# Where the row statistics stand, and how many operand tiles there are: six tiles more, a quarter of the DMA scratch

## The chip, the cores and the metric

The kernel runs on one core of a Trainium2 chip. The metric is device time in microseconds (us) for one execution, from a run of the whole program; 1877.57 us is the median of three runs of the kernel before (1875.49 to 1882.97). On the core, TensorE (PE) multiplies matrices, VectorE (DVE) and ScalarE (ACT) do the elementwise work, GpSimd (POOL) and SyncE (SP) mostly issue DMAs.

## The reference

Five layers in a row on 512 rows of width 1024, all in float32: a SwiGLU feed-forward (ffn1), a mixer of two attentions, a second feed-forward (ffn2), an mLSTM and an RG-LRU, then a last norm. Every layer begins with the same RMS norm and a product with its first weights:

```python
def rms_norm(x, g):
    xf = x.astype(jnp.float32)
    y = xf * lax.rsqrt(jnp.mean(xf * xf, axis=-1, keepdims=True) + EPS)
    return (y * g.astype(jnp.float32)).astype(x.dtype)

def swiglu(x, w_gate, w_up, w_down):
    return (jax.nn.silu(x @ w_gate) * (x @ w_up)) @ w_down

# first block
h = h + 0.5 * swiglu(rms_norm(h, ffn1_norm), ...)
u = rms_norm(h, mix_norm); z = u @ w_in            # two attentions, two gated branches
h = h + merged @ w_out
h = h + 0.5 * swiglu(rms_norm(h, ffn2_norm), ...)
x = rms_norm(h, final_norm)
# second block
x = x + mlstm_mixer(rmsnorm(x, ln_g[0]), ...)
x = x + rglru_mixer(rmsnorm(x, ln_g[1]), ...)
return rmsnorm(x, final_g)

# in mlstm_mixer, of each of 4 heads:
xc = jax.nn.silu(causal_dwconv(xm, conv_w, conv_b))   # 4 taps along the rows
q, k = xc @ w_q, xc @ w_k
v = xm @ w_v
```

## The kernel before

Activations lie transposed: a tile is 128 features by 512 rows. A float32 product is made of three: both sides are split into a rounded part `hi` and a rest `lo`, and `mm3` issues hi·hi (L113), hi·lo (L114) and lo·hi (L115). A `group` is one weight tile of 128x1024 against eight activation tiles, 24 matmuls of 128x512 into one PSUM tile; `bank` and `cbank` are two pools of four such tiles.

The norm is not applied before the first product. `operand` splits x times the gain, without the row factor; the factor 1/rms of each row, spread over all partitions as the tile `rb`, is multiplied in when a product leaves PSUM (L197, L354, L418, L785, L1027). The way to `rb`: `sumsq` squares on ACT, adds on DVE and sums over partitions in four PE matmuls (L171); `rstd` is one DVE instruction (L178) and one power on POOL (L179); `rows` is four PE transposes (L185) and a DVE copy (L187). `stats` does all of that at once, after the first three or four groups of a layer (the mLSTM, which needs two such sums, has the same steps written out after three).

In the feed-forwards most products are done in 256-wide halves by a scheme with fewer products (`xhalves`, `pair_products`): `xhalves` makes seven operands for each of four steps from `x`, the gain and `rb` (L271 to L285). Their weights are sums of weight tiles; one summand comes by an accumulating DMA that POOL issues (L212, 36 of them), all other loads are issued by SP.

In the mLSTM each head needs the convolved, activated input, tile by tile (`x_conv`): one DVE instruction with the first tap (L989), three more (L992), a tanh on ACT (L795), a DVE multiply (L796), then `split`: a cast on ACT (L122) and a subtraction on DVE (L124). The operand, its cast, its rest and the convolution's own temporaries all come out of one pool, `ap`, of tiles of 128x512 float32 with the name `act`: 2 KB in each partition, 34 of them.

The order on each engine is not written out. The framework orders the instructions by priority (offsets of 75 for weights, 100 for evacuations, 200 for `operand`), by the order of the code and by the pools: an instruction that takes a tile from a full pool waits until the last reader of the oldest tile is done, on whatever engine that is. So a pool's size changes the order on all engines. SBUF is full: the pools and the scratch that the program sets aside for the dynamic DMAs (the software ones, which are POOL's) share it.

Of the kernel before, what the change touches and what calls it, by code (L numbers as in the profile page):

```python
# [42 lines left out]
def kernel(ctx: ExitStack, tc: tile.TileContext, a, out):  # L43
    nc = tc.nc
# [1 line left out]

    cp = ctx.enter_context(tc.tile_pool(name="cp", bufs=1))
    op = ctx.enter_context(tc.tile_pool(name="op", bufs=1))
    ap = ctx.enter_context(tc.tile_pool(name="ap", bufs=34))
    wp = ctx.enter_context(tc.tile_pool(name="wp", bufs=5))  # L50
    sp = ctx.enter_context(tc.tile_pool(name="sp", bufs=32))
    gp = ctx.enter_context(tc.tile_pool(name="gp", bufs=2))
# [7 lines left out]
    def act_tile(dt=F32):  # L60
        return ap.tile([P, T], dt, tag="act", name="act")

    def bank():
        return pp.tile([P, T], F32, tag="bank", name="bank")

    def ctile(dt=F32):
        return xp.tile([P, T], dt, tag="chain", name="chain")

    def cbank():
        return qp.tile([P, T], F32, tag="cbank", name="cbank")  # L70

    def small(n):
        return sp.tile([P, 16], F32, tag="small", name="small")[:, :n]

    def f(t):
        return t.bitcast(F32)
# [3 lines left out]
    def vc(name, i=0, n=None):  # L80
        o, w = VEC[name]
        return vec[:, o + i : o + i + (1 if n is None else n)]
# [10 lines left out]
    def wload(src, cols=WU):  # L93
        with tc.high_priority(offset=BOOST):
            raw = wp.tile([P, WU], F32, tag="raw", name="raw", bufs=4)
            nc.sync.dma_start(raw[:, :cols], src)
            hi = wp.tile([P, WU], F32R, tag="hi", name="hi")
            S.copy(hi[:, :cols], raw[:, :cols])  # L98
            lo = wp.tile([P, WU], F32R, tag="lo", name="lo")
            V.tensor_tensor(lo[:, :cols], raw[:, :cols], f(hi[:, :cols]), op=ALU.subtract)  # L100
        return hi, lo
# [10 lines left out]
    def mm3(ps, st, mv, start, stop):  # L112
        PE.matmul(ps, st[0], mv[0], start=start, stop=False)  # L113
        PE.matmul(ps, st[0], mv[1], start=False, stop=False)  # L114
        PE.matmul(ps, st[1], mv[0], start=False, stop=stop)  # L115

    def cut(pair, sl):
        return pair[0][:, sl], pair[1][:, sl]

    def split(x, mk=act_tile):  # L120
        hi = mk(F32R)
        S.copy(hi, x)  # L122
        lo = mk(F32R)
        V.tensor_tensor(lo, x, f(hi), op=ALU.subtract)  # L124
        return hi, lo

    def rowcol(t):
        return t.rearrange("p (r c) -> p r c", c=64)

    def colrow(t):  # L130
        return t.rearrange("p (c r) -> p r c", r=8)

    def operand(x, gain, perm=False):
        xs = []
        for k in range(KD):
            hi, lo = act_tile(F32R), act_tile(F32R)
            xi, hv, lv = (rowcol(x[k]), colrow(hi), colrow(lo)) if perm else (x[k], hi, lo)
            with tc.high_priority(offset=200):
                S.activation(hv, xi, AF.Copy, scale=gain[:, k : k + 1])
                V.scalar_tensor_tensor(lv, xi, gain[:, k : k + 1], f(hv), op0=ALU.mult, op1=ALU.subtract)  # L140
            xs.append((hi, lo))
        return xs

    def group(w, xs, ps=None, start=True, stop=True, base=0):
        if ps is None:
            ps = bank()
        n = len(xs)
        for k in range(n):
            c = (base + k) * P
            mm3(ps, cut(w, slice(c, c + P)), xs[k], start and k == 0, stop and k == n - 1)  # L150
        return ps

    def sumsq(x, perm=False, gain=None, fuse=False):
        acc = None
        for k in range(KD):
            sq = ctile()
            S.activation(sq, x[k], AF.Square, scale=1.0 if gain is None else gain[:, k : k + 1])
            if k == KD - 1:
                if fuse:
                    break  # L160
                t = ctile() if perm else sq
                v = (colrow(t), rowcol(sq), rowcol(acc)) if perm else (t, sq, acc)
                V.tensor_tensor(*v, op=ALU.add)
                sq = t
            elif k:
                V.tensor_tensor(sq, sq, acc, op=ALU.add)
            acc = sq
        ps = cbank()
        for b in range(4):
            c = slice(b * P, (b + 1) * P)  # L170
            PE.matmul(ps[:, b : b + 1], acc[:, c], ones[:, :1], start=True, stop=not fuse)  # L171
            if fuse:
                PE.matmul(ps[:, b : b + 1], sq[:, c], ones[:, :1], start=False, stop=True)
        return ps[:, :4]

    def rstd(ms):
        rs = small(4)
        V.tensor_scalar(rs, ms, 1.0 / D, EPS, op0=ALU.mult, op1=ALU.add)  # L178
        G.tensor_tensor(rs, rs, mhalf[:, :4], op=ALU.pow)  # L179
        return rs  # L180

    def rows(rs):
        ps = cbank()
        for b in range(4):
            PE.transpose(ps[:, b * P : (b + 1) * P], rs[:, b : b + 1].to_broadcast([P, P]), ident)  # L185
        rb = rp.tile([P, T], F32, tag="rb", name="rb")
        V.tensor_copy(rb, ps)  # L187
        return rb

    def stats(x, perm=False):  # L190
        rs = rstd(sumsq(x, perm))
        return rs, rows(rs)

    def silu2(ps, rb):
        g = act_tile()
# [147 lines left out]
    def ffn(x, gain, gu, dn, pre=None):  # L343
        xs = operand(x, gain)
        pre = pre or [wload(gu[0])]
        pre = [group(pre[n] if n < len(pre) else wload(gu[n]), xs, (bank if n < 2 else cbank)()) for n in range(4)]
        _, rb = stats(x)

        def plain(j):
            pg, pu = pre[2 * j : 2 * j + 2] if j < 2 else [group(wload(gu[2 * j + i]), xs) for i in range(2)]  # L350
            s = silu2(pg, rb)
            u = act_tile()
            with tc.high_priority(offset=EVAC):
                V.tensor_tensor(u, pu, rb, op=ALU.mult)  # L354
            V.tensor_tensor(u, u, s, op=ALU.mult)
            return split(u)

        def down(o, w, base, us):
            ps = group(w, us, base=base)
            with tc.high_priority(offset=EVAC):  # L360
                V.scalar_tensor_tensor(x[o], ps, 0.25, x[o], op0=ALU.mult, op1=ALU.add)

        def down_two(o, k0):
            c = slice(k0 * P, k0 * P + T)
            with tc.high_priority(offset=BOOST):
                raw = raw_load([dn[o][:, c], dn[o + 1][:, c]], None)
                return wsplit(raw)

        b, step = xhalves(x, gain, rb)
        pr = [plain(0), plain(1)]  # L370
        for k in range(4):
            step(k)
        pr += [plain(2), plain(3)]
        def down_job(j):

            if j >= 20:
                return lambda i: None
            o, got, us = 2 * (j % 4), [], old

            def step(i):  # L380
                if i < 0:
                    got.append(down_two(o, 4 * (j // 4 - 1)))
                else:
                    down(o + i, got[0], 4 * i, us)

            return step

        cur = Pair(gu[8], gu[9])
        cur.load()
        cur.first()  # L390
        cur.sums()
        cur.last()
        old, new = pr, []
        for j in range(4, KF):
            nxt = Pair(gu[2 * j + 2], gu[2 * j + 3]) if j + 1 < KF else None
            job = down_job(j)
            job(-1)
            new.append(pair_products(cur, b, nxt, job))
            cur = nxt
            if j % 4 == 3 and j < 19:  # L400
                old, new = new, []
        for o in range(KD):
            dw = wload(dn[o][:, 16 * P :], 6 * P)
            down(o, dw, 0, new)
# [4 lines left out]
    def mixer(x):  # L409
        xs = operand(x, vc("gm", 0, 8), perm=True)  # L410
        win = a["win"]
        pre = [group(wload(win[4 * (n % 2) + n // 2]), xs, (bank if n < 2 else cbank)()) for n in range(4)]
        rs, rb = stats(x, perm=True)
        def q_group(i):
            ps = pre[2 * i] if i < 2 else group(wload(win[i]), xs)
            t = act_tile()
# [292 lines left out]
    def mlstm(x):  # L709
        g0 = small(8)  # L710
        V.tensor_tensor(g0, vc("gf", 0, 8), vc("l0", 0, 8), op=ALU.mult)
        xs = operand(x, g0)
        psf = group(wload(a["mif"]), xs, cbank())
        pre = [group(wload(a["mh"][0][j]), xs) for j in range(2)]
        s1 = sumsq(x)
        s2 = sumsq(x, gain=vc("gf", 0, 8))
        rs1 = rstd(s1)
        ms = small(4)
        V.tensor_tensor(ms, rs1, rs1, op=ALU.mult)
        V.tensor_tensor(ms, ms, s2, op=ALU.mult)  # L720
        rs = rstd(ms)
# [3 lines left out]
        rb = rows(rs)  # L725
# [271 lines left out]

    def rglru(x):
        xs = operand(x, vc("l1", 0, 8))
        pre = [group(wload(a["rxr"][j]), xs, (bank if j < 2 else cbank)()) for j in range(3)]  # L1000
        _, rb = stats(x)
        bah, bxh = small(12), small(12)
        V.tensor_scalar(bah, vc("rba", 0, 12), 0.5, None, op0=ALU.mult)
        V.tensor_scalar(bxh, vc("rbx", 0, 12), 0.5, None, op0=ALU.mult)
# [111 lines left out]
    rs = rstd(ms)  # L1116
# [134 lines left out]
```

## Time and profile before

| what | value |
|---|---|
| median of 3 runs | 1877.57 us (1875.49 to 1882.97) |
| profiled execution | 1878.55 us, of which the span is 1876.8 |
| PE busy | 1816.8 us, 97% of the span |
| DVE, ACT, POOL busy | 69%, 42%, 3% |
| granted PE clock, mean | 0.985 of full speed |
| ffn1, mixer, ffn2, mLSTM, RG-LRU | from about 0, 375, 725, 1087 and 1624 us |

The span is the time from the first to the last instruction of the profiled execution, 1.75 us less than its own time. Times in rows count from the span's start. A matmul's row shows its length in the pipeline; what it costs a full engine is the distance from its start to the next one's.

### The profile page before, as it was taken

To read this page: it belongs to the slowest core of one execution; us is meant where nothing else is said; L and a number is where in the kernel's file an instruction comes from. 1 tells how busy PE (TensorE), PEld (TensorE's weight loads), DVE (VectorE), ACT (ScalarE), POOL (GpSimd) and SP (SyncE) were. 2 spreads that over 40 slices of the span, in tenths; PEclk is the share of its full clock that TensorE was granted. 3 is DMA by queue.
4 is the path that set the end of the run, shared out by engine and by line. 5 is a ranking of instruction groups with operands and counts; after the bars stand their busy time and mean duration, and the time that the engine had idled before them with its cause. 6 is when DMAs were issued, how large, how long until landed. Compare 5 with 4: busy or idle time off the path is not lost.

```text
span 1876.8 us, 24687 instructions
## 1 busy us (share of the span) xinstructions
PE 1816.8 (97%) x9616; PEld 1528.2 (81%) x9616; DVE 1287.1 (69%) x2056; ACT 795.4 (42%) x1190; POOL 64.8 (3%) x89
## 2 busy tenths in 40 slices
PE   7999999999999999999999998799999999999998
PEld 5799999877776688799999886687887888888786
DVE  6987778825555464987777766567466466787785
ACT  4443334523344433444333443334334334447662
POOL 0000000000000000000000000000000000000000
PEclk9999999999999999999999999899999999999999
DMA  7265555423321133265555422122222222222212
GB/s 221 85 174 151 152 152 133 143 85 107 96 79 57 57 101 104 68 171 153 152 152 135 127 92 69 55 80 78 78 91 79 79 93 69 95 94 90 87 60 79
DMA packets 74805, 198.09 MB, mean 106 GB/s; under 512 B 8000, under 2 KB 8128, under 8 KB 74688
## 3 DMA queue, kind: packets, MB, share of 16 engines
q1 hardware_dynamic: 63024, 174.35, 28.4%
q0 software_dynamic: 9792, 18.88, 6.3%
q10 hardware_dynamic: 1872, 3.29, 0.6%
q8 instruction: 75, 1.23, 0.3%
q14 instruction: 42, 0.34, 0.1%
HBM read 193.08 MB, written 2.10 MB: 104 GB/s over the span
## 4 chain that ended last, share of the span: by engine, by line
PE 78%; issue 13%; DVE 6%; ACT 2%; DMA 1%; POOL 1%; SPq 0%; POOLq 0%; ACTq 0%; DVEq 0%
PE bank L113 20%; PE bank L114 20%; PE bank L115 19%; PE cbank L114 4%; PE cbank L113 4%; PE cbank L115 4%; PE cbank L869 1%; PE cbank L636 1%; PE cbank L604 1%; DVE act L992 1%; DMA raw<-in_gu_dram 1%; PE cbank L893 1%; ACT hi L98 1%; DVE act L271 1%; PE cbank L894 1%
## 5 line engine op out<-in xcount | busy, mean ns | idle before, releaser
L113 PE MATMUL bank<-act,hi 128*128 128x512 f32 (+1 forms) x1656 | 625.2, 379 | 32.3 <-ACT act L122 24.8
L114 PE MATMUL bank<-act,hi 128*128 128x512 f32 (+1 forms) x1656 | 623.9, 377 | 1.2 <-DVE act L140 0.7
L115 PE MATMUL bank<-act,lo 128*128 128x512 f32 (+1 forms) x1656 | 620.2, 375 | 1.3 <-DVE lo L100 1.3
L98 ACT CAST hi<-raw 128x1024 fp32r<-128x1024 f32 (+2 forms) x211 | 213.3, 1014 | 427.5 <-PE bank L114 241.3
L113 PEld LDWEIGHTS bank<-act,hi 128*128 128x128 f32 x1656 | 316.1, 191 | 93.4 <-ACT act L122 28.2
L114 PEld LDWEIGHTS bank<-act,hi 128*128 128x128 f32 x1656 | 316.2, 191 | 60.0 <-DVE act L124 4.0
L115 PEld LDWEIGHTS bank<-act,lo 128*128 128x128 f32 x1656 | 316.0, 191 | 57.4 <-issue 1.9
L100 DVE TENSOR_TENSOR lo<-raw,hi 128x1024 fp32r<-128x1024 f32 (+2 forms) x211 | 248.1, 1177 | 152.7 <-ACT hi L98 151.8
L218 ACT CAST hi<-raw 128x1024 fp32r<-128x1024 f32 x140 | 146.4, 1050 | 246.8 <-PE cbank L114 108.7
L220 DVE TENSOR_TENSOR lo<-raw,hi 128x1024 fp32r<-128x1024 f32 x140 | 170.6, 1224 | 78.4 <-ACT hi L218 78.4
L113 PE MATMUL cbank<-chain,hi 128*128 128x256 f32 x432 | 123.3, 286 | 2.5 <-ACT chain L122 2.3
L114 PE MATMUL cbank<-chain,hi 128*128 128x256 f32 x432 | 122.9, 285 | 2.2 <-DVE chain L124 2.2
L115 PE MATMUL cbank<-chain,lo 128*128 128x256 f32 x432 | 122.7, 284 | 0.0
L114 PE MATMUL cbank<-act,hi 128*128 128x256 f32 (+1 forms) x264 | 88.2, 334 | 2.2 <-DVE act L124 2.2
L113 PE MATMUL cbank<-act,hi 128*128 128x256 f32 (+1 forms) x264 | 88.5, 335 | 1.5 <-ACT act L122 1.3
L114 PE MATMUL bank<-lo,act 128*128 128x512 f32 x224 | 88.3, 394 | 0.0
L113 PE MATMUL bank<-hi,act 128*128 128x512 f32 x224 | 88.2, 394 | 0.0
L113 PEld LDWEIGHTS cbank<-chain,hi 128*128 128x128 f32 x432 | 83.5, 193 | 5.2 <-ACT chain L122 3.2
L115 PE MATMUL bank<-hi,act 128*128 128x512 f32 x224 | 87.7, 392 | 0.0
L115 PE MATMUL cbank<-act,lo 128*128 128x256 f32 (+1 forms) x264 | 87.7, 332 | 0.0
L114 PEld LDWEIGHTS cbank<-chain,hi 128*128 128x128 f32 x432 | 83.1, 193 | 4.6 <-DVE chain L124 3.1
L115 PEld LDWEIGHTS cbank<-chain,lo 128*128 128x128 f32 x432 | 83.3, 193 | 0.1
(274 smaller groups left out, 2583.1 us busy)
## 6 DMA issues: line engine op xcount, KB each, us to landing
raw<-in_mh_dram SPq DMA_DIRECT2D x64, 512.0 KB, 3.5
raw<-in_gu_dram SPq DMA_DIRECT2D x52, 512.0 KB, 3.6
raw<-in_gu_dram SPq DMA_DIRECT2D x72, 256.0 KB, 2.9
raw<-in_gu_dram POOLq DMA_DIRECT2D x36, 512.0 KB, 6.1
raw<-in_win_dram SPq DMA_DIRECT2D x34, 512.0 KB, 3.5
raw<-in_dn_dram SPq DMA_DIRECT2D x64, 256.0 KB, 2.9
v<-in_gu_dram SPq DMA_DIRECT2D x36, 256.0 KB, 2.8
raw<-in_mo_dram SPq DMA_DIRECT2D x16, 512.0 KB, 3.5
```

The source lines that it names most:

```text
L98: S.copy(hi[:, :cols], raw[:, :cols])
L100: V.tensor_tensor(lo[:, :cols], raw[:, :cols], f(hi[:, :cols]), op=ALU.subtract)
L113: PE.matmul(ps, st[0], mv[0], start=start, stop=False)
L114: PE.matmul(ps, st[0], mv[1], start=False, stop=False)
L115: PE.matmul(ps, st[1], mv[0], start=False, stop=stop)
L218: S.copy(hi, raw)
L220: V.tensor_tensor(lo, raw, f(hi), op=ALU.subtract)
L271: V.scalar_tensor_tensor(t, x[i], gain[:, i : i + 1], rb, op0=ALU.mult, op1=ALU.mult)
L604: PE.matmul(ps[:, :n], bq[i][ro, nb * P : nb * P + P], bk[0][ro, b0 * P : b1 * P], start=True, stop=True)
L636: PE.matmul(po[64 * g : 64 * g + 64, :], bv[0][:, kb * P + 64 * g : kb * P + 64 * g + 64], ptc, start=kb == b0, stop=kb == b1 - 1)
L869: PE.matmul(ps[:, :n], qk[2 + k][:, s * P : s * P + P], qk[k][:, s * P :], start=k == 0, stop=k == 1)
L893: PE.matmul(ps[:, :256], wh, vl[:, c0 : c0 + 256], start=False, stop=False)
```

## The change

`dynamic_dma_scratch_size=4096` is given where nothing was given before (16384 bytes); the 12 KB of each partition that this leaves make six more `act` tiles, 34 to 40. `stats` goes, and `opening` comes: it issues two groups, then the squares and 1/rms, then the third group, then the transposes and the copy, then the fourth group. ffn, mixer and RG-LRU call it (the last made three groups before, and now four); the mLSTM, whose first group is that of its gates, is written out in the same manner, with both of its sums after one more group and then two more groups.

```diff
-    ap = ctx.enter_context(tc.tile_pool(name="ap", bufs=34))
+    ap = ctx.enter_context(tc.tile_pool(name="ap", bufs=40))
...
-    def stats(x, perm=False):
+    def opening(make, x, perm=False):
+
+        gs = [make(0), make(1)]
         rs = rstd(sumsq(x, perm))
-        return rs, rows(rs)
+        gs.append(make(2))
+        rb = rows(rs)
+        gs.append(make(3))
+        return gs, rs, rb
...
         pre = pre or [wload(gu[0])]
-        pre = [group(pre[n] if n < len(pre) else wload(gu[n]), xs, (bank if n < 2 else cbank)()) for n in range(4)]
-        _, rb = stats(x)
+        ws = pre
+        pre, _, rb = opening(lambda n: group(ws[n] if n < len(ws) else wload(gu[n]), xs, (bank if n < 2 else cbank)()), x)
...
-        pre = [group(wload(win[4 * (n % 2) + n // 2]), xs, (bank if n < 2 else cbank)()) for n in range(4)]
-        rs, rb = stats(x, perm=True)
+        pre, rs, rb = opening(lambda n: group(wload(win[4 * (n % 2) + n // 2]), xs, (bank if n < 2 else cbank)()), x, True)
...
         psf = group(wload(a["mif"]), xs, cbank())
-        pre = [group(wload(a["mh"][0][j]), xs) for j in range(2)]
+        pre = [group(wload(a["mh"][0][0]), xs)]
         s1 = sumsq(x)
         s2 = sumsq(x, gain=vc("gf", 0, 8))
+        pre += [group(wload(a["mh"][0][j]), xs) for j in (1, 2)]
...
-        pre = [group(wload(a["rxr"][j]), xs, (bank if j < 2 else cbank)()) for j in range(3)]
-        _, rb = stats(x)
+        pre, _, rb = opening(lambda j: group(wload(a["rxr"][j]), xs, (bank if j < 2 else cbank)()), x)
...
-    nc = bacc.Bacc("TRN2", target_bir_lowering=False, num_devices=1)
+    nc = bacc.Bacc("TRN2", target_bir_lowering=False, num_devices=1, dynamic_dma_scratch_size=4096)
```

Lines of the kernel after are numbered five higher from L197 on: L989, L992, L796, L212 become L994, L997, L801, L217.

On POOL, at the start of ffn1, the kernel before has two accumulating DMAs ahead of the power of `rstd`:

```order
masks.py:199 AFFINE_SELECT ident<-ident 128x128
L212 DMA raw<-in_gu_dram 128x2x512 x2
L179 TENSOR_TENSOR small<-small,mhalf 128x4
L212 DMA raw<-in_gu_dram 128x2x512 x16
L179 TENSOR_TENSOR small<-small,mhalf 128x4
```

The same place in the kernel after:

```order
masks.py:199 AFFINE_SELECT ident<-ident 128x128
L179 TENSOR_TENSOR small<-small,mhalf 128x4
L217 DMA raw<-in_gu_dram 128x2x512 x18
L179 TENSOR_TENSOR small<-small,mhalf 128x4
L588 MEMSET chain 128x384
```

The power stands ahead of all accumulating DMAs of its layer; the number of these is the same. In ffn2 one of them stays ahead of it where there were two. On PE, L171 stands in ffn1 behind 48 matmuls where there were 96, and L185 behind 72 where there were 104.

On DVE, in the mLSTM's first head, the kernel before has its third and fourth convolution tile (each begins with L989) behind the scaling of the attention's transposed columns (L871):

```order
L871 TENSOR_SCALAR chain<-chain,gT 128x128
L989 TENSOR_SCALAR act<-act,vec 128x512 [waits DVE_49,PE_49]
L992 SCALAR_TENSOR_TENSOR act<-act,vec 128x511 [waits DVE_49]
L992 SCALAR_TENSOR_TENSOR act<-act,vec 128x510 [waits DVE_49]
L992 SCALAR_TENSOR_TENSOR act<-act,vec 128x509 [waits DVE_49]
L796 SCALAR_TENSOR_TENSOR act<-act 128x512 [waits Activation_49]
L124 TENSOR_TENSOR act<-act 128x512 [waits PE_49,Activation_49]
L989 TENSOR_SCALAR act<-act,vec 128x512 [waits DVE_49,PE_49]
```

The same two tiles in the kernel after (they begin with L994):

```order
L124 TENSOR_TENSOR act<-act 128x512 [waits Activation_49]
L994 TENSOR_SCALAR act<-act,vec 128x512
L100 TENSOR_TENSOR lo<-raw,hi 128x1024 [waits DMAHW7_49,Activation_49]
L997 SCALAR_TENSOR_TENSOR act<-act,vec 128x511 [waits DVE_49]
L997 SCALAR_TENSOR_TENSOR act<-act,vec 128x510 [waits DVE_49]
L997 SCALAR_TENSOR_TENSOR act<-act,vec 128x509 [waits DVE_49]
L801 SCALAR_TENSOR_TENSOR act<-act 128x512 [waits Activation_49]
L187 COPY rb<-cbank 128x512 [waits PE_49]
L124 TENSOR_TENSOR act<-act 128x512 [waits Activation_49]
L994 TENSOR_SCALAR act<-act,vec 128x512
```

The first instruction of each tile no longer waits for PE, and both tiles stand ahead of the residual's eight scalings (L772, now L777) or among them. The second tile has moved up too: its L994 and its L997s now stand between the scans of the gates (L756 to L759).

On DVE, in the second head, the last of the four convolution tiles before:

```order
L989 TENSOR_SCALAR act<-act,vec 128x512 [waits PE_49]
L992 SCALAR_TENSOR_TENSOR act<-act,vec 128x511 [waits DVE_49]
L992 SCALAR_TENSOR_TENSOR act<-act,vec 128x510 [waits DVE_49]
L863 COPY chain<-cbank 128x512 [waits PE_49]
L992 SCALAR_TENSOR_TENSOR act<-act,vec 128x509 [waits DVE_49]
L871 TENSOR_SCALAR chain<-chain,gT 128x512 [waits DVE_49]
```

and in the kernel after:

```order
L994 TENSOR_SCALAR act<-act,vec 128x512
L997 SCALAR_TENSOR_TENSOR act<-act,vec 128x511 [waits DVE_49]
L997 SCALAR_TENSOR_TENSOR act<-act,vec 128x510 [waits DVE_49]
L997 SCALAR_TENSOR_TENSOR act<-act,vec 128x509 [waits DVE_49]
L801 SCALAR_TENSOR_TENSOR act<-act 128x512 [waits Activation_49]
L124 TENSOR_TENSOR act<-act 128x512 [waits Activation_49]
L868 COPY chain<-cbank 128x512 [waits PE_49]
```

The wait for PE is gone from its first instruction, and the copy from PSUM (L863, now L868) stands behind the whole tile. The third head has the same difference; the fourth had no such wait before. The number of instructions on PE, DVE, ACT, POOL and SP is the same in both kernels.

## Rows read from the trace of the kernel before

**Rows 1.** The page: the span, and busy time of the engines.

```profile
span 1876.8 us, 24687 instructions
...
PE 1816.8 (97%) x9616; PEld 1528.2 (81%) x9616; DVE 1287.1 (69%) x2056; ACT 795.4 (42%) x1190; POOL 64.8 (3%) x89
```

**Rows 2.** Waits of PE, whole span: total us, times, longest us.

```profile
PE bank L113 <- ACT act L122: 24.8, 6, 6.7
...
PE cbank L185 <- POOL small L179: 5.5, 4, 2.6
...
PE cbank L185 <- DVE small L722: 0.9, 1, 0.9
```

**Rows 3.** Timeline, PE, 1159 to 1196: start, length, instruction [idle before <-releaser].

```profile
1159.93 0.48 PE L113 MATMUL bank<-act,hi 128*128 128x512 f32 x1
...
1162.77 0.60 PE L861 MATMUL cbank<-ident,cT 128*128 128x128 f32 x4
1170.08 2.07 PE L113 MATMUL bank<-act,hi 128*128 128x512 f32 x4 [6.71 <-ACT act L122]
...
1179.82 0.80 PE L113 MATMUL bank<-act,hi 128*128 128x512 f32 x1 [4.87 <-ACT act L122]
...
1189.94 0.80 PE L113 MATMUL bank<-act,hi 128*128 128x512 f32 x1 [4.86 <-ACT act L122]
...
1195.09 0.39 PE L113 MATMUL bank<-hi,act 128*128 128x512 f32 x1
```

**Rows 4.** Timeline, DVE, same stretch.

```profile
1162.94 0.54 DVE L989 TENSOR_SCALAR act<-act,vec 128x512 f32<-128x512 f32 x1
...
1174.77 0.55 DVE L989 TENSOR_SCALAR act<-act,vec 128x512 f32<-128x512 f32 x1 [1.88 <-PE bank L114]
```

**Rows 5.** Stages: us, busy PE, PEld, DVE, ACT, POOL, PEclk, DMA, GB/s.

```profile
60.00:76.00 16.00, 12.01 (x62) 9.85 (x62) 15.56 (x29) 8.37 (x15) 0.66 (x1) 0.79 0.11 34
390.00:400.00 10.00, 8.26 (x36) 6.55 (x35) 4.51 (x7) 1.05 (x1) 1.98 (x1) 0.83 0.28 101
770.00:787.00 17.00, 12.71 (x65) 10.90 (x64) 16.20 (x33) 8.33 (x15) 0.25 (x1) 0.80 0.10 32
1145.00:1163.00 18.00, 17.51 (x89) 14.01 (x90) 9.56 (x14) 6.71 (x9) 0.00 (x0) 1.00 0.23 81
1160.00:1198.00 38.00, 21.56 (x63) 14.89 (x61) 23.50 (x36) 13.01 (x21) 1.26 (x8) 0.73 0.09 28
1302.00:1318.00 16.00, 12.09 (x39) 8.37 (x38) 9.23 (x15) 7.83 (x14) 1.59 (x4) 0.79 0.14 40
```

**Rows 6.** Timeline, PE, second head, 1302 to 1316.

```profile
1308.69 0.80 PE L113 MATMUL bank<-act,hi 128*128 128x512 f32 x1 [3.92 <-ACT act L122]
...
1314.17 0.40 PE L113 MATMUL bank<-hi,act 128*128 128x512 f32 x1
```

**Rows 7.** Timeline, DVE, second head.

```profile
1302.79 0.55 DVE L989 TENSOR_SCALAR act<-act,vec 128x512 f32<-128x512 f32 x1 [3.54 <-PE bank L114]
```

**Rows 8.** Timeline, POOL, ffn1.

```profile
36.78 1.21 POOL L212 DMA_DIRECT2D raw<-in_gu_dram  x1 [7.92 <-DMA raw<-in_gu_dram]
37.54 1.52 POOL L179 TENSOR_TENSOR small<-small,mhalf 128x4 f32<-128x4 f32 x1
```

**Rows 9.** Timeline, PE, ffn1.

```profile
39.12 0.65 PE L185 MATMUL cbank<-ident,small 128*128 128x128 f32 x4 [2.61 <-POOL small L179]
```

**Rows 10.** Timeline, DVE, ffn1.

```profile
39.81 0.69 DVE L187 COPY rb<-cbank 128x512 f32<-128x512 f32 x1 [3.93 <-PE cbank L185]
...
51.72 1.41 DVE L271 SCALAR_TENSOR_TENSOR act<-h,vec,rb 128x512 f32<-128x512 f32 x2
```

**Rows 11.** Instructions of line L212: its DMAs' time to landing.

```profile
DMA to landing us min/median/max: 5.7/6.1/9.2
```

**Rows 12.** Timeline, POOL, ffn1's products.

```profile
120.10 1.20 POOL L212 DMA_DIRECT2D raw<-in_gu_dram  x1 [10.56 <-DVE lo L220]
```

**Rows 13.** Timeline, ACT, same place.

```profile
127.47 1.05 ACT L218 CAST hi<-raw 128x1024 fp32r<-128x1024 f32 x1 [3.03 <-PE bank L114]
```

## The prediction

> **What bounds the kernel now.** I read the page's busy times first. PE is busy for 1816.8 of 1876.8 us [rows 1]; the next engine has 69%. So the chain of work is PE's, and its idle 60 us are what an edit of order can win, with one addition: what PE's clock loses around the idle. Second I read who PE waits for [rows 2]. The reader is to see how few waits there are: six for a cast of an operand tile on ACT (L122) hold 24.8 us, four for the power of the row statistics on POOL 5.5, one more in the mLSTM's opening 0.9. Third, the timeline where the long ones stand: three of 6.71, 4.87 and 4.86 us in the mLSTM's first head, each ahead of one convolution tile's 12 matmuls [rows 3], and one of 3.92 in the second head [rows 6]; the third head repeats it. Last, the table of stages [rows 5]: in the two feed-forward openings (60 to 76 and 770 to 787) DVE is busy for 15.56 of 16 and 16.20 of 17 us while PE stands for 3.99 and 4.29, so there PE waits for the seven operands of each half step, which DVE makes too late.
>
> The clock stands in the same table. [...] In matmuls: twelve at the full clock took from 1159.93 to 1162.77, 0.237 us each [rows 3]; the 36 of the three tiles took 4.87, 5.26 and 5.15 us between the waits (each end is the next start less its wait), 15.28 where 36 x 0.237 make 8.53. So the first head loses 16.44 by waits and 6.75 by the clock, 23.2 us. The second loses 3.92 and (5.48 from 1308.69 to 1314.17, less 12 x 0.237) 2.64, together 6.6 [rows 6], and the third as much.
>
> **The convolution tiles (pool of 40).** Why the casts are late: the tile's first DVE instruction, L989, waits for PE [rows 4, 7]. The tile it writes belongs to PE's last reader of an older one, so a tile's convolution begins when the matmuls of the tile before end, and its chain of about 5 us (1174.77 to 1179.82) stands open to PE. The arithmetic is unchanged; with six more tiles that wait is gone in the new order, and the second to fourth tile move up. What comes late next is DVE's own time. One tile costs it 0.55 + 2.32 + two of 0.69, some 4.2 us. Two tiles move into the stretch before 1163, where DVE is busy for 9.56 of 18 us [rows 5]: 8.4 us of work meet 8.4 us of room, a full fit. The second stands between the gates' scans, so PE's transposes of these are late by up to its four instructions, about 2.8 us; in the order they stand behind some ten more matmuls (2.4 us), so nearly nothing of that shows. The fourth tile shares DVE with the residual; laid one behind the other, its cast ends at about 1168.6 and its rest at 1169.8, and PE, which goes on at 1162.8 with 36 matmuls of 0.237, wants them at about 1168.6 and 1169. I take 22 of the 23.2 us; the bounds are 16.4 (the waits go, the clock doesn't come back) and 23.2. In the second head DVE can begin the last tile where its 3.54 us of idle began, 1299.25 [rows 7]: three L992 after it, tanh, multiply and cast bring the cast to about 1304.1, the rest to 1304.9. PE gets there at 1304.2 (its transposes L861 now stand behind). I take 6.0 of 6.6 us, and the same in the third: 12 us, bounds 7.8 and 13.2.
>
> [...]
>
> **The openings.** The edit removes no instruction; it moves the chain from the squares to `rb` ahead of one or two groups, and draws one RG-LRU group ahead of the evacuations. In ffn1 the chain was held twice: L171 stood behind four whole groups, and the power stood on POOL behind an accumulating DMA that waited for its own load until 36.78 [rows 8]; PE then waited 2.61 us [rows 9]. Now L185 stands 32 matmuls earlier (7.6 us) and the power ahead of the DMAs, so `rb` is done about 10 us sooner than 39.81 [rows 10]. Queued behind the power on POOL is now the layer's first accumulating DMA; the power is done before 30 by this, and the DMA waited for its load anyway. The first half step (L271) began 11.9 us after `rb` [rows 10], behind evacuations, some of which still wait for PE's groups; I let the steps come 8 to 10 us sooner. PE reaches their products 2.6 us sooner, so of the 3.99 us of waits I keep 1.5, and of the clock's part 0.5: the low clock lasted 0.21 x 16 x 2 = 6.7 us, some 5 of them busy, which cost 2.5. Gain: 2.6 + 2.5 + 2.0 = 7.1, of which I take 6.1, because the weights' splits (L220) are pushed behind the steps on a full DVE; bounds 2.6 and 9.1. ffn2: waits of 4.29, and 2.5 for a low clock of the same length (0.20 x 17 x 2 = 6.8); I take 5.3 of 6.8, bounds 2 and 6.8. Mixer: 1.74 us idle (390 to 400 [rows 5]) and half of the 3.4 us at the low clock (0.17 x 10 x 2), 1.7; the sums stand far ahead in the new order: 3.4, bounds 1.7 and 3.4. The four waits for POOL hold 5.5 us [rows 2]; ffn1's 2.61 and the mixer's 1.74 leave 1.15 for those of ffn2 and RG-LRU: I take 1.1, bounds -1 and 2, since DVE has one group more to evacuate late in RG-LRU. mLSTM: its wait of 0.9 goes [rows 2], bounds 0 and 1.4.
>
> **The scratch.** 36 DMAs use it, and POOL is busy for 3% [rows 1]. No trace here shows a smaller one. They land after 6.1 us [rows 11] and follow each other at 12 us and more in the products (10.56 us of idle ahead of one [rows 12]), so one is under way at a time. I take 0, the row nearest to it being that idle. From both sides: -1 us, if less is to be set up, and, if it holds each DMA, the third rival's price. [...]
>
> **The sum.** 22 + 12 + 6.1 + 5.3 + 3.4 + 1.1 + 0.9 + 0 = 50.8 us off the profiled execution's 1878.55 (1876.8 of span [rows 1] and 1.75 around it): 1827.8. The median shown is 1.0 lower, inside the runs' own spread of 7; I say 1828. By the lower bounds (16.4 + 7.8 + 2.6 + 2 + 1.7 - 1 + 0) the gain is 29.5, by the upper ones (23.2 + 13.2 + 9.1 + 6.8 + 3.4 + 2 + 1.4 + 1) 60.1: 1818 to 1849.
>
> **Rivals.**
> 1. DVE takes the place of the pool. The first head's room is an exact fit by my count, and DVE is full in both ffn openings. If the second to fourth tile each come 2 us late, PE still waits 6 us there, and if the ffn openings win only the wait for POOL and half of the rest, the sum falls to 16 + 12 + 4 + 3 + 3.4 + 1 = 39.4: 1839. For: DVE at 97% in those stages. Against: the new order has no PE waits in those tiles.
> [...]
> 3. Slower: the smaller scratch holds POOL. The place is L212's issue in the two ffns' products. A DMA issued at 120.10 [rows 12] lands by the median at 126.2, and the next cast of weights (L218) begins at 127.47, held by PE and not by the load [rows 13]: 1.3 us of cover. If each of 36 issues is held by h, PE loses 36 x (h - 1.3). That eats the 51 us from h = 2.7 on; at half a landing, 3.05, it costs 63, and the time is 1878.6 - 50.8 + 63 = 1891. For: no row bounds it. Against: POOL has 10 us of idle between its issues.
> 4. The change doesn't do what it says: tiles weren't the limit, and the waits come back behind other readers. Only the openings then win: 16, 1862. Against: the order.
>
> **How the numbers follow.** Forecast 0.57 (its own range 1820 to 1837), first rival 0.15, second 0.14, third 0.07, fourth 0.03; 0.04 for no change, if gains and a small loss by POOL cancel. About 0.5%, 9 us, is what a measurement can tell from no change. Faster: 0.57 + 0.15 + 0.14 + 0.03 = 0.89; same 0.04; slower 0.07. The range goes past the second rival, 1817 to 1855, and leaves out the third, the fourth and no change.
>
> **What would show it.** In the profile after: no wait of PE for ACT L122 over 1 us between 1130 and 1440, a granted clock of 0.95 or more in the stages of the three heads; `rb` of ffn1 (L187) near 30 us; no PE wait for POOL; ffn stages with under 2 us of PE idle; the accumulating DMAs' landing still at 6 us. DMA rows of several us on POOL, or casts on ACT that wait for `raw`, would speak for the third rival. If the first head still shows waits of 2 us and more behind a full DVE, my fit in [rows 5] was wrong.

## The result and the profile after

The kernel after takes 1818.35 us (median of 4 runs, 1817.53 to 1819.43), against 1878.03 of the kernel before (4 runs, 1875.49 to 1882.97): a ratio of 0.968, 95% interval 0.966 to 0.970. 59.7 us are gone, where 50 were forecast; the time lies inside the range of 1817 to 1855, 1.4 us above its low end, and 1.7 below the narrower range of 1820 to 1837 that the forecast gave itself. The spread of the runs has shrunk too, from 7.5 to 1.9 us.

The page of the kernel after, busy times, to be read beside [rows 1]:

```profile
span 1816.1 us, 24639 instructions
...
PE 1793.5 (99%) x9616; PEld 1514.2 (83%) x9616; DVE 1286.3 (71%) x2056; ACT 793.8 (44%) x1190; POOL 67.3 (4%) x89
```

PE does the same 9616 matmul rows. The span is 60.7 us shorter: PE's idle time fell by 37.4 (from 60.0 to 22.6) and its busy time by 23.3, since matmuls at the low clock are longer rows (a row of L115 in the trace of before took 0.63 us at 1172.38, at a granted clock of 0.50, and 0.39 at 1174.57, at 1.00); the mean granted clock went from 0.985 to 0.999. DVE, ACT and POOL are as busy as they were.

Who PE waits for, the longest and, last, the one that was the longest before [rows 2]:

```profile
PE bank L113 <- ACT act L139: 6.9, 1, 6.9
PE bank L483 <- DVE act L480: 1.9, 1, 1.9
PE cbank L114 <- DVE act L124: 1.0, 2, 0.5
...
PE bank L113 <- ACT act L122: 0.2, 1, 0.2
```

The first is the program's start, the second a wait in the mixer that the change leaves alone. The six waits for L122 with 24.8 us have become one of 0.2, and the four for POOL's power are no longer in the list.

The stages of the kernel after that answer to [rows 5]: ffn1's products, the mixer's opening, ffn2's products, the stretch before the first head's last tiles, the first head and the second. Columns as there.

```profile
56.00:72.00 16.00, 14.32 (x89) 11.92 (x88) 16.00 (x27) 8.84 (x14) 0.00 (x0) 1.00 0.33 100
380.00:390.00 10.00, 10.00 (x47) 8.34 (x46) 5.53 (x7) 1.96 (x2) 0.00 (x0) 1.00 0.25 68
756.00:772.00 16.00, 14.12 (x87) 11.69 (x86) 15.80 (x27) 8.92 (x13) 0.00 (x0) 1.00 0.31 95
1125.00:1143.00 18.00, 17.64 (x87) 13.79 (x86) 16.02 (x25) 10.16 (x15) 0.00 (x0) 1.00 0.24 79
1135.00:1165.00 30.00, 30.00 (x132) 23.17 (x131) 24.79 (x39) 16.98 (x30) 1.70 (x8) 1.00 0.23 73
1258.00:1274.00 16.00, 16.00 (x71) 12.09 (x70) 9.41 (x18) 9.19 (x18) 2.09 (x4) 1.00 0.22 67
```

The granted clock is 1.00 in all of them, and in the last two, the heads, PE has no idle. DVE is busy for 16.02 us of the stretch 1125 to 1143 where it had 9.56 [rows 5]: the second and third convolution tile stand there now, and 2 us of room are left where the forecast counted none. DVE is still full in the products of the feed-forwards, and PE is still idle for 1.7 and 1.9 us there.

DVE in the first head, the beginnings of the second, third and fourth convolution tile and the rest of the fourth, which answer to [rows 4]:

```profile
1125.26 0.54 DVE L994 TENSOR_SCALAR act<-act,vec 128x512 f32<-128x512 f32 x1
...
1134.31 0.54 DVE L994 TENSOR_SCALAR act<-act,vec 128x512 f32<-128x512 f32 x1
...
1141.52 0.54 DVE L994 TENSOR_SCALAR act<-act,vec 128x512 f32<-128x512 f32 x1
...
1149.19 0.68 DVE L124 TENSOR_TENSOR act<-act 128x512 fp32r<-128x512 f32 x1
```

and PE at that fourth tile, which answers to [rows 3]:

```profile
1148.66 1.20 PE L113 MATMUL bank<-act,hi 128*128 128x512 f32 x4
1149.70 0.27 PE L866 MATMUL cbank<-ident,cT 128*128 128x128 f32 x1
1149.93 0.50 PE L114 MATMUL bank<-act,hi 128*128 128x512 f32 x1
```

None of the four DVE rows has a bracket: DVE is not idle ahead of them, and neither is PE ahead of the matmuls that read the tile. The last tile's rest ends at 1149.87 and the first matmul that reads it (L114) starts at 1149.93. It is a close fit, as forecast, but PE's order has four L113, which read only the cast, and a transpose to do first.

In ffn1, POOL, PE and DVE, which answer to [rows 8 to 10] (three timelines):

```profile
23.87 1.34 POOL L179 TENSOR_TENSOR small<-small,mhalf 128x4 f32<-128x4 f32 x1 [22.48 <-DVE small L178]
26.70 1.38 POOL L217 DMA_DIRECT2D raw<-in_gu_dram  x1 [1.49 <-DMA raw<-in_gu_dram]
```

```profile
28.96 0.60 PE L185 MATMUL cbank<-ident,small 128*128 128x128 f32 x4
```

```profile
29.60 0.69 DVE L187 COPY rb<-cbank 128x512 f32<-128x512 f32 x1 [4.14 <-PE cbank L185]
...
43.16 1.41 DVE L276 SCALAR_TENSOR_TENSOR act<-h,vec,rb 128x512 f32<-128x512 f32 x2
```

POOL's power is through before the first DMA is issued, `rb` is done 10.2 us sooner, and the half steps begin 8.6 us sooner. The accumulating DMAs land as before [rows 11]:

```profile
DMA to landing us min/median/max: 5.8/5.9/7.9
```

To see where the time went I compared the start of the n-th matmul row in both traces. What each stretch gained in us, beside the terms of the forecast (its 1.1 for the power of ffn2 and RG-LRU is shared out, 0.4 and 0.7):

| stretch | forecast | measured |
|---|---|---|
| ffn1 opening | 6.1 | 7.5 |
| mixer opening | 3.4 | 3.5 |
| mixer, behind its wait at 491 | 0 | 1.5 |
| mixer, 585 to 655 | 0 | 0.8 |
| ffn2 opening (with its power) | 5.7 | 5.7 |
| mLSTM opening | 0.9 | 1.1 |
| first head | 22 | 23.4 |
| second and third head | 12 | 13.7 |
| RG-LRU opening | 0.7 | 0.95 |
| RG-LRU, rest | 0 | 2.6 |

The table compares one execution with one. How far a row of it holds shows in a second execution of the old order, that of the scratch alone (among the experiments below; its profiled time is 1882.6 us where the kernel before had 1878.55). Against the kernel before it loses 2.6 us more in ffn1's opening, 1.3 more in the first head and 1.6 more late in RG-LRU, and 1.5 less behind the mixer's wait. The stages 36 to 50 and 1825 to 1840 of the kernel before:

```profile
36.00:50.00 14.00, 11.39 (x53) 9.15 (x52) 8.91 (x14) 3.90 (x5) 2.28 (x2) 1.00 0.30 52
1825.00:1840.00 15.00, 13.20 (x58) 10.31 (x57) 13.68 (x20) 6.09 (x9) 0.00 (x0) 1.00 0.31 105
```

and of the scratch alone:

```profile
36.00:50.00 14.00, 10.70 (x43) 8.53 (x42) 6.90 (x10) 2.83 (x4) 2.28 (x2) 0.88 0.22 41
1825.00:1840.00 15.00, 13.21 (x51) 10.15 (x50) 13.42 (x19) 7.21 (x11) 0.00 (x0) 0.89 0.20 58
```

In the first stage PE waits for POOL, 2.61 us and 3.30; in the second it is idle for 1.8 us in both. Behind these waits the clock fell in one execution and stayed at 1.00 in the other. So a row of the table can be off by 1 to 3 us where the old order has waits.

### The profile page after: what moved, and what is told of

Its sections match the earlier page's. It is cut to its first block, busy times and chain, and to the rows that moved or that the text cites. A ratio compares the mean times of both kernels' runs of the same rounds, so it can differ in the third digit from the quotient of the medians.

```text
span 1816.1 us, 24639 instructions
## 1 busy us (share of the span) xinstructions
PE 1793.5 (99%) x9616; PEld 1514.2 (83%) x9616; DVE 1286.3 (71%) x2056; ACT 793.8 (44%) x1190; POOL 67.3 (4%) x89
## 4 chain that ended last, share of the span: by engine, by line
PE 80%; issue 13%; DVE 4%; ACT 1%; DMA 1%; SPq 0%; POOLq 0%; POOL 0%; ACTq 0%; DVEq 0%
PE bank L113 20%; PE bank L114 20%; PE bank L115 20%; PE cbank L113 4%; PE cbank L115 4%; PE cbank L114 4%; PE cbank L874 1%; PE cbank L640 1%; PE cbank L608 1%; DVE act L276 1%; PE cbank L897 1%; PE cbank L898 1%; PE cbank L899 1%; PE cbank L577 0%; DMA raw<-in_gu_dram 0%
## 5 line engine op out<-in xcount | busy, mean ns | idle before, releaser
L113 PE MATMUL bank<-act,hi 128*128 128x512 f32 (+1 forms) x1648 | 615.1, 375 | 8.4 <-ACT act L139 6.9
L114 PE MATMUL bank<-act,hi 128*128 128x512 f32 (+1 forms) x1648 | 614.8, 373 | 1.5 <-DVE act L124 0.8
L115 PE MATMUL bank<-act,lo 128*128 128x512 f32 (+1 forms) x1648 | 613.0, 372 | 0.3 <-DVE lo L100 0.3
L113 PEld LDWEIGHTS bank<-act,hi 128*128 128x128 f32 x1648 | 310.8, 189 | 67.6 <-ACT act L139 6.9
L114 PEld LDWEIGHTS bank<-act,hi 128*128 128x128 f32 x1648 | 311.2, 189 | 57.8 <-DVE act L124 3.5
L115 PEld LDWEIGHTS bank<-act,lo 128*128 128x128 f32 x1648 | 311.1, 189 | 55.2 <-issue 1.9
L114 PE MATMUL cbank<-chain,hi 128*128 128x256 f32 x432 | 122.4, 283 | 0.9 <-DVE chain L124 0.9
L113 PE MATMUL cbank<-chain,hi 128*128 128x256 f32 x432 | 122.2, 283 | 0.0
L115 PE MATMUL cbank<-chain,lo 128*128 128x256 f32 x432 | 122.2, 283 | 0.0
L113 PE MATMUL cbank<-act,hi 128*128 128x256 f32 (+1 forms) x272 | 91.5, 337 | 0.3 <-ACT act L122 0.3
L114 PE MATMUL cbank<-act,hi 128*128 128x256 f32 (+1 forms) x272 | 90.8, 334 | 1.0 <-DVE act L124 1.0
L115 PE MATMUL cbank<-act,lo 128*128 128x256 f32 (+1 forms) x272 | 90.6, 333 | 0.0
L113 PE MATMUL bank<-hi,act 128*128 128x512 f32 x224 | 87.7, 391 | 0.0
L115 PE MATMUL bank<-hi,act 128*128 128x512 f32 x224 | 87.4, 390 | 0.0
L114 PE MATMUL bank<-lo,act 128*128 128x512 f32 x224 | 87.2, 389 | 0.0
L114 PEld LDWEIGHTS cbank<-chain,hi 128*128 128x128 f32 x432 | 82.7, 191 | 2.8 <-DVE chain L124 1.3
L113 PEld LDWEIGHTS cbank<-chain,hi 128*128 128x128 f32 x432 | 82.7, 191 | 2.0 <-ACT chain L122 0.5
L115 PEld LDWEIGHTS cbank<-chain,lo 128*128 128x128 f32 x432 | 82.7, 191 | 0.5
```

## The experiments

**Each half alone.** The tiles and the scratch without the openings:

```diff
-    ap = ctx.enter_context(tc.tile_pool(name="ap", bufs=34))
+    ap = ctx.enter_context(tc.tile_pool(name="ap", bufs=40))
...
-    nc = bacc.Bacc("TRN2", target_bir_lowering=False, num_devices=1)
+    nc = bacc.Bacc("TRN2", target_bir_lowering=False, num_devices=1, dynamic_dma_scratch_size=4096)
```

> Half of the change: 40 operand tiles and the scratch of 4096 bytes; the row statistics are issued where the kernel before has them. Theory (the two halves act in different places and add up): the PE waits for ACT's casts in the mLSTM's three heads and the low clock behind them go, 23.6 + 6.7 + 7.0 us by the two traces, so some 37 us less, up to 41 if the tiles also won the 4.5 us that the traces show outside the heads and the openings: 1837 to 1841 us; the openings of the feed-forwards keep their 4 us of idle PE each and the low clock. Rival (DVE was relieved by the earlier statistics, and without that it has no room for the convolution tiles): less than half of it, 1860 or more.

It took 1838.2 us (ratio 0.978, 0.977 to 0.980). PE's waits for POOL, and the stages of ffn1's products and of the first head, in that order:

```profile
PE cbank L185 <- POOL small L179: 5.9, 4, 3.0
```

```profile
60.00:76.00 16.00, 12.11 (x58) 9.75 (x58) 15.33 (x32) 8.09 (x14) 0.00 (x0) 0.79 0.10 34
1155.00:1195.00 40.00, 40.00 (x204) 32.70 (x203) 31.43 (x68) 18.98 (x32) 1.69 (x8) 1.00 0.23 79
```

The first head is cured (40 of 40 us busy, clock 1.00) and the opening is as it was (clock 0.79 [rows 5]). The time lies in the 1837 to 1841 expected. The rival, that DVE needed the earlier statistics to have room, falls.

The openings without tiles and scratch:

```diff
-    ap = ctx.enter_context(tc.tile_pool(name="ap", bufs=40))
+    ap = ctx.enter_context(tc.tile_pool(name="ap", bufs=34))
...
-    nc = bacc.Bacc("TRN2", target_bir_lowering=False, num_devices=1, dynamic_dma_scratch_size=4096)
+    nc = bacc.Bacc("TRN2", target_bir_lowering=False, num_devices=1)
```

> The other half: the row statistics between the first four groups; 34 operand tiles and the default scratch as before. Theory: the openings win what the two traces show there (7.5 ffn1, 3.5 mixer, 5.6 ffn2, 1.1 mLSTM, 1 RG-LRU), some 19 us, up to 23 with the 4.5 us elsewhere: 1855 to 1859 us; the three waits of 5 to 7 us in the first head and the one in the second and third stand as before. Rival (with 34 tiles the earlier statistics find no tiles, and the steps of the feed-forwards stay late): only the wait for POOL and the mixer's go, 6 us, 1872.

It took 1859.05 us (0.989, 0.988 to 0.991). PE's waits for the cast, and the same two stages:

```profile
PE bank L113 <- ACT act L122: 24.8, 6, 6.7
```

```profile
56.00:72.00 16.00, 14.13 (x89) 11.80 (x88) 15.89 (x27) 8.95 (x14) 0.00 (x0) 1.00 0.31 100
1140.00:1180.00 40.00, 23.56 (x77) 16.54 (x76) 25.10 (x38) 13.77 (x22) 1.26 (x8) 0.74 0.11 39
```

Here the openings are cured and the heads are not. The ratios multiply to 0.9783 x 0.9894 = 0.968, that of the whole change: the halves act in different places and add up. The 2.6 us late in RG-LRU are the tiles': that stretch gains 2.6 with the tiles alone. With the openings alone it loses 1.6, as it does with the scratch alone, where the clock of the stage behind an old wait is 0.89 (above).

**The scratch.** The kernel before with `dynamic_dma_scratch_size=4096` alone; the order is the same on every engine.

```diff
-    nc = bacc.Bacc("TRN2", target_bir_lowering=False, num_devices=1)
+    nc = bacc.Bacc("TRN2", target_bir_lowering=False, num_devices=1, dynamic_dma_scratch_size=4096)
```

> The kernel before with the scratch of 4096 bytes alone, 34 tiles, and the same order on every engine. Theory (about one accumulating DMA is under way at a time): 1878 us, within 3, with the DMAs landing after 6 us and POOL's issues of 1.2 us. [...]

1880.05 us against 1880.66, ratio 1.000 (0.999 to 1.001). And the changed kernel with a quarter of its scratch:

```diff
-    nc = bacc.Bacc("TRN2", target_bir_lowering=False, num_devices=1, dynamic_dma_scratch_size=4096)
+    nc = bacc.Bacc("TRN2", target_bir_lowering=False, num_devices=1, dynamic_dma_scratch_size=1024)
```

> The changed kernel with a quarter of its scratch again, 1024 bytes, same order on every engine. Theory: each accumulating DMA is issued more than 10 us after the one before, which lands in 6, so even room for little more than one costs nothing: 1818 us, within 3. Rival: POOL waits for room at each issue; if it is held by 3.05 us, half a landing, the time rises by up to 63 us, to 1881; if it waits only where two follow closely (the first two of a feed-forward), 1818 to 1822.

1817.43 us, ratio 0.967 (0.965 to 0.969), that of the change. POOL's DMA issues in it (count: min/median/max in ns) and their landing:

```profile
L217 POOL DMA_DIRECT2D raw<-in_gu_dram x36: 1203/1219/1378, 27.0 to 993.7; - x36
...
DMA to landing us min/median/max: 5.7/5.8/8.1
```

No issue is held, at a quarter or at a sixteenth of the room before: with 4096 bytes, and in the kernel before, the issues take 1203/1203/1378 ns. The slower rival of the prediction had a price but no cause here.

**How many tiles.** 38 and 36 in place of 40, all else as in the change.

```diff
-    ap = ctx.enter_context(tc.tile_pool(name="ap", bufs=40))
+    ap = ctx.enter_context(tc.tile_pool(name="ap", bufs=38))
```

> 38 operand tiles. In the order only the fourth convolution tile of the first head begins with a wait for PE. Theory: the fourth tile's chain stands open, 1818 plus 3 to 7, 1821 to 1825, and not better than 36 tiles for sure, since what counts is which tile waits. Rival (even growth): a third of 41 is lost, 1832.

1824.61 us (0.970, 0.969 to 0.972), 6.3 above the change. PE's waits for the cast:

```profile
PE bank L113 <- ACT act L122: 5.1, 2, 4.9
```

One wait of 4.9, ahead of the fourth tile and nowhere else, costs 6.7 in that stretch: the tile that the order shows waiting, and the low clock behind it (0.94 in the stage 1143 to 1170, where the change has 1.00). With 36:

```diff
-    ap = ctx.enter_context(tc.tile_pool(name="ap", bufs=40))
+    ap = ctx.enter_context(tc.tile_pool(name="ap", bufs=36))
```

> The changed kernel with 36 operand tiles in place of 40 (scratch 4096, same openings). In its order only the third convolution tile of the first head still begins with a wait for PE; the second and third head have none. Theory (each tile that still waits for PE's matmuls costs one chain of about 5 us and the low clock behind it, 2.3): 1818 plus up to 7, 1821 to 1826. Rival (the gain grows evenly with the tiles, 41 us over six): two thirds of 41 are lost, 1845.

1827.95 us (0.972, 0.971 to 0.974), 9.6 above the change, and 2.0 above the top of the 1821 to 1826 that I expected:

```profile
PE bank L113 <- ACT act L122: 6.0, 2, 5.8
```

The wait is 5.8, ahead of the third tile, and the head's stretch loses 8.9. Some 1.8 more is lost at and behind the mixer's wait at 480, which is 2.2 us long where the change has 1.9 and has a low clock behind it (0.89 in the stage 474 to 490, in the change 1.00). The old order had a like loss there in one execution and not in another, so this part isn't shown to come from the tiles. All six tiles are worth 40.7 us (1859.05 with the openings alone, less 1818.35). With four of them 6.3 are missing, with two 9.6: the gain does not grow evenly with the tiles (that would have made 1832 and 1845), but hangs on each wait that a tile takes away, and the first two take most of them.

**What in the opening counts.** The power stays early on POOL, but the transposes and `rb` go behind the fourth group again:

```diff
         gs = [make(0), make(1)]
         rs = rstd(sumsq(x, perm))
-        gs.append(make(2))
-        rb = rows(rs)
-        gs.append(make(3))
+        gs += [make(2), make(3)]
+        rb = rows(rs)
```

> The changed kernel, but the transposes and the copy to rb stand behind the fourth group again in ffn, mixer and RG-LRU; the squares and the power stay behind the second group (POOL's power ahead of the DMAs). Theory (when rb is ready sets the feed-forward steps; the wait for POOL is the smaller part): the waits for POOL stay away, and the feed-forward openings lose part of their gain, about 3 us each, 1823 to 1826. Rival (POOL's queue was the whole matter): 1818, as the change.

1827.79 us (0.972, 0.971 to 0.974), 9.4 above the change and 1.8 above the top of the 1823 to 1826 expected: 5.1 are lost in ffn1 and 5.1 in ffn2 by the traces. PE waits for POOL no more. `rb`, the first half step, and the stage of ffn1's products:

```profile
35.07 0.69 DVE L187 COPY rb<-cbank 128x512 f32<-128x512 f32 x1 [2.09 <-PE cbank L185]
...
48.77 1.41 DVE L275 SCALAR_TENSOR_TENSOR act<-h,vec,rb 128x512 f32<-128x512 f32 x2
```

```profile
54.00:70.00 16.00, 12.10 (x56) 9.86 (x55) 16.00 (x33) 7.40 (x14) 0.00 (x0) 0.79 0.03 12
```

So POOL's queue is the smaller part (with the power early and `rb` late, 2.4 of the 7.5 us in ffn1 stay won and 0.6 of the 5.7 in ffn2): the waits behind DVE and the clock of 0.79 are back because `rb` is 5.5 us later. The mixer and RG-LRU lose nothing by it. The other way, one step further:

```diff
-        gs = [make(0), make(1)]
+        gs = [make(0)]
         rs = rstd(sumsq(x, perm))
-        gs.append(make(2))
+        gs.append(make(1))
         rb = rows(rs)
-        gs.append(make(3))
+        gs += [make(2), make(3)]
```

> A step further in the change's direction: the squares and the power behind the first group, the transposes behind the second. Theory (DVE is full in the feed-forward openings, and what is left of PE's waits there is 1.6 us each): rb comes some 5 us sooner, and of the 1.6 us in each feed-forward about half goes, 1816 to 1818. Rival (the squares' matmuls then wait for DVE's sums, which are not ready so early): one to two us more, 1819 to 1821.

1812.21 us (0.964, 0.962 to 0.965), 6.1 below the change and below the 1816 to 1818 expected: the fastest of these kernels.

```profile
24.64 0.69 DVE L187 COPY rb<-cbank 128x512 f32<-128x512 f32 x1 [1.02 <-PE cbank L185]
...
38.63 1.41 DVE L276 SCALAR_TENSOR_TENSOR act<-h,vec,rb 128x512 f32<-128x512 f32 x2
```

```profile
54.00:70.00 16.00, 15.95 (x102) 14.28 (x101) 15.44 (x24) 7.82 (x11) 0.25 (x1) 1.00 0.29 100
```

`rb` and the first half step lie 13.6, 13.7 and 14.0 us apart in the change and in these two (11.9 in the kernel before); when `rb` moves, the steps move, and PE's waits with them. At 24.64 the steps are ahead of PE. The gain is 2.6 us in ffn1 and 3.1 in ffn2. That is more than PE's idle there in the change, 1.7 and 1.9, which its timeline explains (PE, ffn1):

```profile
58.54 0.28 PE L114 MATMUL cbank<-chain,hi 128*128 128x256 f32 x1
58.66 0.28 PE L115 MATMUL cbank<-chain,lo 128*128 128x256 f32 x1
59.09 0.38 PE L113 MATMUL cbank<-act,hi 128*128 128x256 f32 x1 [0.15 <-ACT act L122]
59.98 0.38 PE L114 MATMUL cbank<-act,hi 128*128 128x256 f32 x1 [0.50 <-DVE act L124]
```

The last starts 0.89 us after the one before, where such matmuls start 0.12 apart without a wait (58.54 and 58.66): 0.77 lost, of which the bracket shows 0.50. Such a wait costs more here than its idle, since the row of the matmul ahead of it counts as busy until its end (0.38 us, to 59.47), part of which lies under the next matmul when nobody waits (the row at 58.54 is 0.28 us long, and the next one starts at 58.66). Over the whole stage, the matmuls behind a wait start 3.95 us after the ones before them, where some 1.1 would do: 2.9 us lost with 1.7 of idle, and 2.6 came back.

## Why the prediction was right, and where it was short

The forecast's mechanism held in each part. The tiles' waits went as the order showed, DVE had room for three moved tiles, and my end of the fourth tile's rest (1169.8 in the time of the kernel before, which is 20.1 later than that of the kernel after at that place, so 1149.7) came at 1149.87. The clock came back with them (1.00 in the stages of the heads), so the second rival, in which it stays low and the 18.3 us that the sum has from it (6.8 + 5.3 + 2 + 2.5 + 1.7) are not won, 1846 us,, is out; DVE took the pool's place nowhere in the heads, so the first is out as well; the scratch costs nothing (ratio 1.000, 0.999 to 1.001).

The sum was 9 us short, in the sizes of its terms, and the time fell below the forecast's own 1820 to 1837:

- I gave the heads 34 and they gained 37.1. I had taken 1.2 off the first for a late rest and 0.6 off each of the others; PE's order has matmuls on the cast alone at those places, and the stretches gained the whole loss that the rows of before showed, and a little more.
- The ffn1 opening gained 7.5, not 6.1. The forecast kept 1.5 us of waits, and 1.7 stayed, so the discount of 1.0 for weight splits behind the steps doesn't seem to have been needed; but against the execution of the scratch alone the same opening gains 10.1, so this term can't be read to 1 us.
- I left out RG-LRU's later stretch (2.6) and one in the mixer (0.8), which the tiles gained (both are gained with the tiles alone). RG-LRU's waits were in the trace of before as single waits of 0.3 to 1.3 us; I priced only the large groups.
- The 1.5 us in the mixer are not the change's. The kernel before lost them to the low clock behind its wait at 491; with the scratch alone, the same order, the same wait and no low clock. The stage 485 to 501 of the kernel before, and of that kernel:

```profile
485.00:501.00 16.00, 14.20 (x77) 10.89 (x76) 8.88 (x22) 5.08 (x13) 0.00 (x0) 0.89 0.31 100
```

```profile
485.00:501.00 16.00, 14.24 (x84) 10.65 (x83) 10.47 (x24) 5.85 (x13) 0.00 (x0) 1.00 0.41 132
```

PE is idle there for 1.8 us in both.

That the clock's loss goes with the waits was the author's estimate from [rows 5], where the stages with waits have a clock of 0.73 to 0.83 and the one without has 1.00. It held for the waits that went: the stages that answer to these have 1.00 in the kernel after. As a reading of every wait it was too simple, also in the trace of before: behind ffn1's wait of 2.61 us for POOL the clock stayed at 1.00, and behind waits of 1.3 to 1.8 us it fell in one execution and not in the other.

The factor of 2 in the forecast's lengths of the low clock (6.7, 6.8 and 3.4 us, from which its 2.5, 2.5 and 1.7 come) stands in none of its rows, but in the same trace: in windows of half a us the granted clock is 1.00 or 0.50 in all but 19 of 3752, and the low stretches of ffn1, ffn2 and the mixer's opening are 6.8, 6.8 and 3.4 us long by these.

The upper bounds of the terms made 60.1 us together, and the gain was 59.7. That these agree is luck: by the table the listed terms gained 55.8, and 4.9 came that I hadn't listed, 1.5 of them not by the change. The discounts for leftovers in the heads and the terms left out were the error.

## What to carry to other kernels

When an engine is busy for 97% and the rest is a few waits of several us, read what the first instruction of the late chain waits for: if it is a reader of an old tile, one more buffer can be worth a whole chain, and the number that matters is the one at which that wait leaves the order, not the average over buffers. Start the chain that everything behind a layer's opening needs as early as its inputs allow, and then try one step earlier still. Add to each long wait what the clock lost behind it (here some 2.3 us for the 12 matmuls behind one of 5 us), and to short waits the overlap that they take away (here 2.9 us lost for 1.7 of idle).

## What was not expected

Behind a wait of 1.8 us the clock was low in one execution (0.89) and not in another of the same order (1.00); no run shows what decides it. In ffn1 it went the other way, with the wait of 2.6 us in the kernel before at the full clock, and that of 3.3 with the scratch alone in a stage (36 to 50) of 0.88. In the trace of before the low clock stands only behind idle of PE (ten stretches, each with 1.7 us or more of it in the 8 us before), but not each wait brings it. With the waits gone, so is the spread: 13 runs of the kernel before lay between 1874.73 and 1882.96, 4 of the kernel after within 1.9 us.
